# MLP weight factors of a fast pair made in place in its two raw buffers, in another order

## The chip, the cores and the metric

The kernel runs on one core of a Trainium2 chip. The time is that of one execution on the device in microseconds (us). It was measured three times for the kernel before: 2042.0, 2046.69 and 2047.65 us, with a median of 2046.69. Next to these stands one execution that was profiled.

Engine names in the profile: PE is TensorE (matmuls), PEld its weight loads, DVE is VectorE, ACT is ScalarE, POOL is GpSimd and SP is SyncE, which issues the loads. L145 is line 145 of the kernel.

## What is computed

A trunk of two layers over 256 tokens of width 2048. The first has a gated short convolution as its mixer, the second a latent attention; each is followed by a squared-ReLU MLP, and every part ends in a layer norm of the weighted residual sum. The change lies in the MLPs alone:

```python
def sq_relu_mlp(x, w1, w2):
    return jnp.square(jax.nn.relu(x @ w1)) @ w2

for layer in range(DEPTH):            # 2
    ...
    h = layer_norm(ALPHA * h + mix, ln_g[layer, 0], ln_b[layer, 0])
    h = layer_norm(ALPHA * h + sq_relu_mlp(h, mlp_w1[layer], mlp_w2[layer]),
                   ln_g[layer, 1], ln_b[layer, 1])
```

`w1` is 2048 x 8192 and `w2` 8192 x 2048, both float32.

## The kernel before

**Number form.** TensorE works on rounded floats (`F32R`). A float32 weight tile is therefore split in two: `hi` is the rounded value (a cast on ScalarE, L144), `lo` is the rest (source minus `hi`, on VectorE, L145). The function `split` does both. A product of two split operands is three matmuls (`dot`, L296 to L298): hi by hi, lo by hi, hi by lo.

**The stream of weights.** All weights of the kernel come in one list, `stream`, in the order of their use. An entry of kind "unit" is one tile of 128 x 1024 (512 KB). `prepare(i)` makes entry i ready: it loads it into a raw buffer (`load_raw`, a DMA on SyncE's queue, L165) and splits it into a pair of hi and lo buffers (`parts`). There are RAW = 5 raw buffers of 4 KB per partition and WA = 8 pairs of hi and lo. `take` hands out the next entry and first runs `prepare` so far that eight slots are ahead; a unit fills one slot, a plain pair two, a fast pair three.

**The second product of the MLP.** For 28 of the 32 pairs of K tiles (K is the 8192-wide inner dimension), `h @ w2` is made by a seven-product scheme for 2 x 2 blocks, in two column halves b = 0 and 1. A *fast pair* is one K tile pair in one half. Its weights come as two tiles: the first holds the blocks 11 and 22, the second 21 and 12. From them four factors are made:

- T1 = b12 - b11 and T3 = b12 - b22, in one VectorE instruction of 1024 columns into a third raw buffer `t` (L195)
- T2 = b22 - T1, in place of b12 (L197)
- T4 = b21 - T2, in place of b11, once b11 has been split (L199)

The tiles (11, 22), (T1, T3) and (21, T2) are then split into one hi/lo slot each, and T4 by itself into a tile `t4_i` of the tag "t4", which has two buffers of 4 KB. The three `yield` of `prepare` are the borders of the three slots. 92 pairs are fast, 46 in each layer; the others (`PLAIN`) are used as they are, with eight products and two slots.

**Seven sums in PSUM banks.** `FAST` lists the products as (sum, left factor, right factor), and a group of 21 matmuls runs them in that order; `PLAINS` does the same for a plain pair, with sums 3, 1, 2, 4 first. The sums 1 to 7 stay in seven PSUM banks while pairs of one half follow one another. After every four pairs the other half is taken up: `turn` spills each bank to SBUF (`spill`, ScalarE copy, L585) and puts the other half's sum back (`seed`, ScalarE copy, L589), bank by bank in the order of `FAST`, 1 3 7 5 2 6 4. With a plain pair next, bank 1 gets the sum "C" instead. The eighth bank is the only one left for the next item.

**Between the pairs**, one block of `x @ w1` (two units, 32 matmuls L231 and L235 into `ps_m`) is made after each group. ScalarE and VectorE empty it (`whole`, L337 and L338); after every second one they apply ReLU and square (L723, L659), form sums of blocks (L666 to L669) and split the result (`hc`, `ha`).

**What sets the order.** The source is one program order. A planner in the compiler draws up the queue of each engine from it: an instruction is placed when, by the planner's costs, its inputs are there, its buffer has been given back and its engine is free, earlier ones of the program first. [...] A buffer of a tag is given back when the last instruction that reads it has run.

Of the kernel before, what the change touches and what calls it, by code (L numbers as in the profile page):

```python
# [9 lines left out]
F32 = mybir.dt.float32  # L10
F32R = mybir.dt.float32r
AF = mybir.ActivationFunctionType
ALU = mybir.AluOpType
AX = mybir.AxisListType

P = 128
# [12 lines left out]
RMS_EPS = 1e-6  # L29
SCALE = (128 + 64) ** -0.5  # L30
NEG = -1e30
RAW, WA = 5, 8
NB = 4
BW = D // NB
PAIRS = FF // (2 * P)
# [13 lines left out]
def trunk(ctx: ExitStack, tc: tile.TileContext, xT, vecs, w_in, w_out, w_kv, w_q, w_uk, w_uv,  # L49
          w_qn, w_qp, w_o, w1, w2, w2f, cosT, sinT, mask, ident, gb, out):  # L50
    nc = tc.nc
# [3 lines left out]
    raws = ctx.enter_context(tc.tile_pool(name="raws", bufs=RAW))  # L55
# [83 lines left out]
    state = {"made": 0, "next": 0}  # L139
    ready = {}  # L140

    def split(hi, lo, src):

        nc.scalar.copy(hi, src)  # L144
        nc.vector.tensor_tensor(lo, src, hi.bitcast(F32), ALU.subtract)  # L145

    def tiled(w):
        return w.rearrange("p (b c) -> p b c", c=P)

    def parts(i):  # L150
        return tuple(whl.tile([P, 8, P], F32R, tag=t, name=f"{t}{i}") for t in ("hi", "lo"))
# [11 lines left out]
    def load_raw(i, src):  # L163
        raw = raws.tile([P, 1024], F32, tag="raw", name=f"raw{i}")
        nc.sync.dma_start(raw, src)  # L165
        return raw

    def prepare(i):

        kind, *src = stream[i]  # L170
        if kind == "unit":
            raw = load_raw(i, src[0])
            hi, lo = ready[i] = parts(i)
            split(hi, lo, tiled(raw))
            yield
            return
        r1, r2 = (load_raw(f"{i}_{j}", v) for j, v in enumerate(src))

        def finished(r, name):
            w = parts(f"{i}_{name}")  # L180
            split(*w, tiled(r))
            return [[v.rearrange("p b c -> p (b c)")[:, o:o + BW] for v in w] for o in (0, BW)]

        b11, b22, b21, b12 = r1[:, :BW], r1[:, BW:], r2[:, :BW], r2[:, BW:]
        out = {}
        if kind == "plain":
            out["11"], out["22"] = finished(r1, 1)
            yield
            out["21"], out["12"] = finished(r2, 2)
            ready[i] = out  # L190
            yield
            return
        t = raws.tile([P, 1024], F32, tag="raw", name=f"raw{i}_t")
        two = "p (a c) -> p a c"
        nc.vector.tensor_tensor(t.rearrange(two, a=2), b12.unsqueeze(1).to_broadcast([P, 2, BW]),  # L195
                                r1.rearrange(two, a=2), ALU.subtract)
        nc.vector.tensor_tensor(b12, b22, t[:, :BW], ALU.subtract)  # L197
        out["11"], out["22"] = finished(r1, 1)
        nc.vector.tensor_tensor(b11, b21, b12, ALU.subtract)  # L199
        yield  # L200
        out["T1"], out["T3"] = finished(t, "t")
        yield
        out["21"], out["T2"] = finished(r2, 2)
        f = state["fast"].tile([P, 2, BW], F32R, tag="t4", name=f"t4_{i}", bufs=2)
        split(f[:, 0, :], f[:, 1, :], b11)
        out["T4"] = [f[:, 0, :], f[:, 1, :]]
        ready[i] = out
        yield

    def all_steps():  # L210
        for i in range(2 * GROUP, len(stream)):
            yield from prepare(i)
# [319 lines left out]
    for m in range(NC):  # L532
        part = []
        for what in "cub":
            ps = next(pss)
            f = cbuf[:, m % 2, "cub".index(what), :T]
            whole(ps, f)
            part.append(f)
            if what == "u":
# [4 lines left out]
                y = cbuf[:, m % 2, 4, :T]  # L544
# [5 lines left out]
        if m >= NC // 2:  # L550
# [3 lines left out]
    ln.widen("a1", "a2")  # L554
    summed(ln, products(NC, z), residual)

    FAST = (("1", "11", "11"), ("3", "S4", "22"), ("7", "S3", "T3"), ("5", "S1", "T1"),
            ("2", "12", "21"), ("6", "S2", "T2"), ("4", "22", "T4"))
    PLAINS = (("3", "12", "22"), ("1", "22", "22"), ("2", "11", "11"), ("4", "21", "11"),
              ("3", "11", "12"), ("1", "21", "12"), ("2", "12", "21"), ("4", "22", "21"))  # L560

    class Sums:
# [30 lines left out]
        def group(self, b, w, x, plain, last, turns):  # L593
            forms = PLAINS if plain else FAST
            done = [p for p, _, _ in forms]
            for i, (p, l, r) in enumerate(forms):
                new = p not in self.live
                if p not in self.bank:
                    pool = pmm if p < "5" else Banks.more
                    self.bank[p] = pool.tile([P, 512], F32, tag="mm", name=f"sum{p}")  # L600
                dot(self.bank[p], w[r], x[l], new,
                    p not in done[i + 1:] and (last or p == "1" and turns), True)
                self.live[p] = (b, "C" if p == "1" and plain else p)

        def turn(self, b, plain):

            for p, _, _ in FAST:
                if p in self.bank:
                    self.spill(p)
                    self.seed(p, (b, "C" if p == "1" and plain else p))  # L610
# [184 lines left out]
    with tc.tile_pool(name="att", bufs=1) as ap:  # L795
# [61 lines left out]
        f = tmp.tile([P, T], F32, tag="fh", name="fpe", bufs=3)  # L857
# [28 lines left out]
        with tc.tile_pool(name="att2", bufs=2) as a2, \  # L886
# [73 lines left out]
            def attention(g, box):  # L960
                gens = [attend(4 * g + j, box) for j in range(4)]
                for step in range(6):
                    for j in range(3, -1, -1):
                        if 0 <= step - j < 3:
                            next(gens[j])
                            yield
# [14 lines left out]
            for g in range(5):  # L981
                box = {}
                a = attention(g - 1, prev) if prev is not None else iter(())
# [147 lines left out]
```

## Time and profile before

| | |
|---|---|
| runs (us) | 2042.0, 2046.69, 2047.65; median 2046.69 |
| profiled execution (us) | 2041.95 |
| its span (us) | 2040.0 |
| TensorE busy | 2003.0 us, 98% of the span |
| weight loads busy | 1740.1 us, 85% |
| VectorE busy | 1717.1 us, 84% |
| ScalarE busy | 1386.8 us, 68% |
| DMA | 385.31 MB, mean 189 GB/s |

The span runs from the first to the last instruction of the program. Busy times are unions, so overlapping instructions of one engine count once. A matmul's end is modelled, and matmuls overlap: a busy TensorE is not one at its peak, and the distance from one start to the next says more than the duration. Rows of groups read: line, engine, operation, output <- inputs, shape, count | busy us, mean ns of one | idle us of that engine just before them, and what ended most of it. Rows of waits read: who waited <- whom: us in all, times, longest. Idle time of an engine that is not the bottleneck costs nothing by itself.

### The profile page before, as it was taken

To read this page: it belongs to the slowest core of one execution; us is meant where nothing else is said; L and a number is where in the kernel's file an instruction comes from. 1 tells how busy PE (TensorE), PEld (TensorE's weight loads), DVE (VectorE), ACT (ScalarE), POOL (GpSimd) and SP (SyncE) were. 2 spreads that over 40 slices of the span, in tenths; PEclk is the share of its full clock that TensorE was granted. 3 is DMA by queue.
4 is the path that set the end of the run, shared out by engine and by line. 5 is a ranking of instruction groups with operands and counts; after the bars stand their busy time and mean duration, and the time that the engine had idled before them with its cause. 6 is when DMAs were issued, how large, how long until landed. Compare 5 with 4: busy or idle time off the path is not lost.

```text
span 2040.0 us, 30047 instructions
## 1 busy us (share of the span) xinstructions
PE 2003.0 (98%) x11088; PEld 1740.1 (85%) x11088; DVE 1717.1 (84%) x2483; ACT 1386.8 (68%) x2071; POOL 2.3 (0%) x21
## 2 busy tenths in 40 slices
PE   9999999999999999999999999999999999999997
PEld 8888888988888888888889998898788888888886
DVE  7667677799889898898878888779898988989886
ACT  6444444687887788877756655568777788787761
POOL 0000000000000000000000000000000000000000
PEclk9999999999999999999999999999999999999999
DMA  8655556455565665665754544655656666666672
GB/s 300 206 191 189 189 187 187 158 175 194 188 204 190 203 202 181 200 202 187 238 174 150 167 128 125 202 164 160 203 190 206 197 197 191 197 203 191 201 236 102
DMA packets 108003, 385.31 MB, mean 189 GB/s; under 512 B 11984, under 2 KB 13392, under 8 KB 107856
## 3 DMA queue, kind: packets, MB, share of 16 engines
q1 hardware_dynamic: 107712, 383.13, 58.1%
q8 instruction: 87, 1.43, 0.3%
q14 instruction: 60, 0.49, 0.1%
q10 hardware_dynamic: 144, 0.26, 0.0%
HBM read 381.25 MB, written 2.10 MB: 188 GB/s over the span
## 4 chain that ended last, share of the span: by engine, by line
PE 61%; DVE 18%; DMA 10%; ACT 6%; issue 4%; DVEq 0%; SPq 0%; ACTq 0%
PE ps_u L231 13%; PE ps_m L231 9%; DMA raw<-in_w2f_dram 9%; PE ps_u L235 7%; DVE lo L145 6%; PE ps_m L235 4%; PE sum L296 3%; PE sum L298 3%; PE sum L297 3%; ACT hi L144 3%; DVE raw_t L195 2%; DVE lo_t L145 2%; DVE ha L145 2%; PE ps_d L296 1%; PE ps_d L298 1%
## 5 line engine op out<-in xcount | busy, mean ns | idle before, releaser
L145 DVE TENSOR_TENSOR lo<-raw,hi 128x1024 fp32r<-128x1024 f32 x712 | 857.0, 1220 | 173.4 <-ACT hi L144 92.2
L144 ACT CAST hi<-raw 128x1024 fp32r<-128x1024 f32 x712 | 743.6, 1053 | 374.3 <-PE ps_u L231 157.7
L231 PE MATMUL ps_m<-xhl,hi 128*128 128x512 f32 x1792 | 455.1, 393 | 2.9 <-DVE sf L338 2.8
L231 PEld LDWEIGHTS ps_m<-xhl,hi 128*128 128x128 f32 x1792 | 330.1, 189 | 70.6 <-DVE sf L338 6.2
L235 PEld LDWEIGHTS ps_m<-xhl,lo 128*128 128x128 f32 x1792 | 245.2, 190 | 18.1
L235 PE MATMUL ps_m<-xhl,lo 128*128 128x256 f32 x1792 | 250.9, 282 | 0.0
L296 PE MATMUL sum<-hi,hc 128*128 128x512 f32 x512 | 202.6, 396 | 7.3 <-ACT sum L589 7.3
L297 PE MATMUL sum<-lo,hc 128*128 128x512 f32 x512 | 200.7, 392 | 0.0
L298 PE MATMUL sum<-hi,ha 128*128 128x512 f32 x448 | 173.3, 390 | 0.0
L231 PE MATMUL ps_u<-xhl_a,hi 128*128 128x512 f32 x720 | 172.0, 391 | 0.0
L144 ACT CAST hi_t<-raw_t 128x1024 fp32r<-128x1024 f32 x92 | 97.0, 1055 | 93.4 <-DVE raw_t L195 85.0
L231 PEld LDWEIGHTS ps_u<-xhl_a,hi 128*128 128x128 f32 x720 | 132.4, 188 | 25.7
L195 DVE TENSOR_TENSOR raw_t<-raw,raw 128x1024 f32<-128x1024 f32 x92 | 112.5, 1223 | 46.9 <-DMA raw<-in_w2f_dram 46.2
L296 PEld LDWEIGHTS sum<-hi,hc 128*128 128x128 f32 x512 | 96.6, 189 | 29.7 <-ACT sum L589 13.0
L585 ACT COPY sums<-sum 128x512 f32<-128x512 f32 x204 | 118.5, 587 | 3.5 <-PE sum L298 2.6
L589 ACT COPY sum<-sums 128x512 f32<-128x512 f32 x186 | 111.5, 599 | 1.4
L145 DVE TENSOR_TENSOR lo_t<-raw_t,hi_t 128x1024 fp32r<-128x1024 f32 x92 | 112.1, 1219 | 0.0
L297 PEld LDWEIGHTS sum<-lo,hc 128*128 128x128 f32 x512 | 96.7, 189 | 15.3
L298 PEld LDWEIGHTS sum<-hi,ha 128*128 128x128 f32 x448 | 84.2, 188 | 18.5
L235 PEld LDWEIGHTS ps_u<-xhl_a,lo 128*128 128x128 f32 x720 | 92.3, 191 | 3.5
L235 PE MATMUL ps_u<-xhl_a,lo 128*128 128x256 f32 x720 | 93.4, 283 | 0.0
L296 PE MATMUL sum<-hi_t,hc 128*128 128x512 f32 x168 | 66.5, 396 | 10.5 <-ACT sum L589 10.4
(241 smaller groups left out, 3315.7 us busy)
## 6 DMA issues: line engine op xcount, KB each, us to landing
raw<-in_w_dram SPq DMA_DIRECT2D x288, 512.0 KB, 4.5
raw<-in_w2f_dram SPq DMA_DIRECT2D x224, 512.0 KB, 4.0
raw<-in_w_in_dram SPq DMA_DIRECT2D x90, 512.0 KB, 4.3
raw<-in_w_out_dram SPq DMA_DIRECT2D x32, 512.0 KB, 4.0
raw<-in_w_o_dram SPq DMA_DIRECT2D x32, 512.0 KB, 3.7
raw<-in_w_kv_dram SPq DMA_DIRECT2D x10, 512.0 KB, 3.9
raw<-in_w_q_dram SPq DMA_DIRECT2D x8, 512.0 KB, 4.3
raw<-in_w_uk_dram SPq DMA_DIRECT2D x8, 512.0 KB, 4.4
```

What stands on the lines that cost most here:

```text
L144: nc.scalar.copy(hi, src)
L145: nc.vector.tensor_tensor(lo, src, hi.bitcast(F32), ALU.subtract)
L195: nc.vector.tensor_tensor(t.rearrange(two, a=2), b12.unsqueeze(1).to_broadcast([P, 2, BW]), r1.rearrange(two, a=2), ALU.subtract)
L231: nc.tensor.matmul(ps, w[blk // 8][0][:, blk % 8, :], x, start=first, stop=False)
L235: nc.tensor.matmul(ps[:, :T], w[blk // 8][1][:, blk % 8, :], x[:, :T], start=False, stop=last)
L296: nc.tensor.matmul(ps, x[0], w[0], start=first, stop=False, skip_group_check=goes_on)
L297: nc.tensor.matmul(ps, x[0], w[1], start=False, stop=False, skip_group_check=goes_on)
L298: nc.tensor.matmul(ps, x[1], w[0], start=False, stop=last, skip_group_check=goes_on)
L585: nc.scalar.copy(self.slot(self.live.pop(p)), self.bank[p])
L589: nc.scalar.copy(self.bank[p], self.at(key))
```

## The change

The four factors are made without the third raw buffer, by four subtractions of 512 columns, all after the split of the first tile:

- T1 = b12 - b11 in place of b11, T3 = b12 - b22 in place of b12, T2 = b22 - T1 in place of b22; these stand in the first slot's share of the program
- (T1, T2) is split from the first tile's buffer; then T4 = b21 - T2 in place of b11 and its split; these are the second slot's share
- (21, T3) is split from the second tile's buffer in the third slot's share

The tag "t4" has one buffer instead of two, and there are six raw buffers instead of five; the SBUF in use stays the same. The products of a fast group run in the order 1 3 5 6 4 2 7, and a turn goes by the same order if a fast pair is next, and by 1 3 4 2 5 6 7 if a plain one is.

```diff
-RAW, WA = 5, 8
+RAW, WA = 6, 8
...
-        t = raws.tile([P, 1024], F32, tag="raw", name=f"raw{i}_t")
-        two = "p (a c) -> p a c"
-        nc.vector.tensor_tensor(t.rearrange(two, a=2), b12.unsqueeze(1).to_broadcast([P, 2, BW]),
-                                r1.rearrange(two, a=2), ALU.subtract)
-        nc.vector.tensor_tensor(b12, b22, t[:, :BW], ALU.subtract)
+        minus = lambda o, x, y: nc.vector.tensor_tensor(o, x, y, ALU.subtract)
         out["11"], out["22"] = finished(r1, 1)
-        nc.vector.tensor_tensor(b11, b21, b12, ALU.subtract)
+        minus(b11, b12, b11)
+        minus(b12, b12, b22)
+        minus(b22, b22, b11)
         yield
-        out["T1"], out["T3"] = finished(t, "t")
-        yield
-        out["21"], out["T2"] = finished(r2, 2)
-        f = state["fast"].tile([P, 2, BW], F32R, tag="t4", name=f"t4_{i}", bufs=2)
+        out["T1"], out["T2"] = finished(r1, "t")
+        minus(b11, b21, b22)
+        f = state["fast"].tile([P, 2, BW], F32R, tag="t4", name=f"t4_{i}", bufs=1)
         split(f[:, 0, :], f[:, 1, :], b11)
         out["T4"] = [f[:, 0, :], f[:, 1, :]]
+        yield
+        out["21"], out["T3"] = finished(r2, 2)
         ready[i] = out
         yield
...
-    FAST = (("1", "11", "11"), ("3", "S4", "22"), ("7", "S3", "T3"), ("5", "S1", "T1"),
-            ("2", "12", "21"), ("6", "S2", "T2"), ("4", "22", "T4"))
+    FAST = (("1", "11", "11"), ("3", "S4", "22"), ("5", "S1", "T1"), ("6", "S2", "T2"),
+            ("4", "22", "T4"), ("2", "12", "21"), ("7", "S3", "T3"))
...
-            for p, _, _ in FAST:
+            for p in "1342567" if plain else [p for p, _, _ in FAST]:
                 if p in self.bank:
                     self.spill(p)
                     self.seed(p, (b, "C" if p == "1" and plain else p))
```

## The prediction

> **What bounds the kernel now.** I read the busy time of each engine by stretches (engines in the order PE, PEld, DVE, ACT, POOL, then TensorE's clock, the DMA share and GB/s), then who waits for whom.
>
> ```profile
> 440.00:1010.00 570.00, 558.54 (x2826) 471.27 (x2825) 517.26 (x623) 445.02 (x628) 0.00 (x0) 1.00 0.60 197
> ...
> 1390.00:1975.00 585.00, 575.35 (x2913) 486.33 (x2912) 529.97 (x636) 460.65 (x653) 0.00 (x0) 1.00 0.62 198
> ...
> PE sum L296 <- ACT sum L589: 18.0, 18, 2.5
> PE ps_m L231 <- DVE sf L338: 2.8, 2, 2.3
> ```
>
> These two stretches are the fast products of the two MLPs, where the edited code runs. TensorE idles there 570.0 - 558.5 = 11.5 and 585.0 - 575.4 = 9.7 us, and nearly all of it has two names: the first matmul of a product waiting for ACT to put a sum back into its bank (18.0 us in 18 waits), and a w1 product waiting for VectorE to empty its one bank (2.8 in 2). Weights are not named there. TensorE is the bound, and can save little more than these waits.
>
> A wait costs more than its idle time, as the timeline shows (start, duration, engine, line, idle time before in brackets):
>
> ```profile
> 810.54 0.39 PE L298 MATMUL sum<-hi_t,ha 128*128 128x512 f32 x1
> 812.85 0.50 PE L296 MATMUL sum<-hi_t,hc 128*128 128x512 f32 x1 [1.92 <-ACT sum L589]
> 813.18 0.40 PE L297 MATMUL sum<-lo_t,hc 128*128 128x512 f32 x1
> 813.42 0.39 PE L298 MATMUL sum<-hi_t,ha 128*128 128x512 f32 x1
> ...
> 480.00:520.00 40.00, 37.70 (x188) 31.83 (x187) 34.51 (x44) 31.41 (x45) 0.00 (x0) 0.96 0.63 203
> 1440.00:1480.00 40.00, 36.99 (x178) 30.73 (x177) 34.23 (x42) 30.47 (x43) 0.00 (x0) 0.96 0.58 188
> ```
>
> Undisturbed, a 512-column matmul starts about 0.23 us after the one before (813.18 to 813.42 is 0.24). At this wait 2.31 pass instead of 0.23, and then 0.33: 0.26 more than the 1.92 idle. For 20 waits that is 5.2 us. In two stretches of 40 us the granted clock is 0.96: 0.04 x 40 = 1.6 us each, 3.2 together. **Ceiling** of what waits can give back: 18.0 + 2.8 + 5.2 + 3.2 = 29 us.
>
> Why is ACT late? Its timeline in that wait, and the busy times and waits of a steady stretch of the first MLP, 520 to 1000 us (total us, times, longest):
>
> ```profile
> 810.50 1.05 ACT L144 CAST hi<-raw 128x1024 fp32r<-128x1024 f32 x1 [0.96 <-PE sum L298]
> 811.45 0.58 ACT L585 COPY sums<-sum 128x512 f32<-128x512 f32 x1
> ...
> 812.19 0.60 ACT L589 COPY sum<-sums 128x512 f32<-128x512 f32 x1
> ...
> 520.00:1000.00 480.00, 471.00 (x2385) 397.29 (x2384) 434.37 (x515) 380.92 (x539) 0.00 (x0) 1.00 0.61 198
> ...
> ACT hi L144 <- DMA raw<-in_w2f_dram: 23.3, 25, 2.3
> DVE raw_t L195 <- DMA raw<-in_w2f_dram: 20.8, 24, 2.1
> DVE lo L145 <- ACT hi L144: 16.8, 27, 1.5
> ...
> ACT hi L144 <- PE ps_m L231: 7.0, 9, 1.2
> ...
> SPq L165 <- DVE lo L145: 168.1, 97, 5.6
> SPq L165 <- DVE lo_t L145: 142.1, 33, 6.4
> ```
>
> The seed that TensorE wants ends at 812.8, behind a cast that itself waited and a spill, in one queue. In 480 us ACT is busy 380.9 and VectorE 434.4, and both lose time to the same thing: w2 tiles that have not landed (23.3 and 20.8 us). The loads are late because SyncE waits for VectorE to give raw buffers back. So the loop behind ACT's lateness is the five raw buffers.
>
> **The change part by part.**
>
> *VectorE's arithmetic.*
>
> ```profile
> L195 DVE TENSOR_TENSOR raw_t<-raw,raw 128x1024 f32<-128x1024 f32 x92 | 112.5, 1223 | 46.9 <-DMA raw<-in_w2f_dram 46.2
> L145 DVE TENSOR_TENSOR lo_t<-raw_t,hi_t 128x1024 fp32r<-128x1024 f32 x92 | 112.1, 1219 | 0.0
> L199 DVE TENSOR_TENSOR raw<-raw 128x512 f32<-128x512 f32 x92 | 63.3, 688 | 1.4
> L197 DVE TENSOR_TENSOR raw<-raw,raw_t 128x512 f32<-128x512 f32 x92 | 63.2, 687 | 1.2
> L145 DVE TENSOR_TENSOR t<-raw,t 128x512 fp32r<-128x512 f32 x92 | 63.0, 685 | 1.6 <-ACT t L144 1.6
> L144 ACT CAST hi_t<-raw_t 128x1024 fp32r<-128x1024 f32 x92 | 97.0, 1055 | 93.4 <-DVE raw_t L195 85.0 <-PE ps_m L231 5.4 <-PE ps_m L235 2.5
> L144 ACT CAST t<-raw 128x512 fp32r<-128x512 f32 x92 | 57.3, 623 | 7.1 <-DVE raw L199 7.1
> ```
>
> Per fast pair it removes one 1024-wide subtraction and two 512-wide (1.223 + 0.687 + 0.688 = 2.598 us) and adds four 512-wide of the same form (4 x 0.688 = 2.752): +0.154 us, x92 = +14.2 us of VectorE's time. The cover is VectorE's idle time: 480.0 - 434.4 = 45.6 us in the steady stretch, against 38 pairs x 0.154 = 5.9 (38: the 92 pairs shared out over the 570 + 585 us by time). On the path: 0. If the cover were gone it would cost the whole 14.2. Splits stay as they are in number and size; so do DMAs and matmuls.
>
> *Raw buffers.* Before, a step (fast pair plus one w1 block) takes 3 + 2 = 5 of 5 raw buffers; after, 2 + 2 = 4 of 6.
>
> ```profile
> 494.68 0.40 PE L296 MATMUL sum<-hi,hc 128*128 128x512 f32 x1
> ...
> 499.46 1.98 PE L231 MATMUL ps_m<-xhl,hi 128*128 128x512 f32 x8
> ...
> 505.02 0.40 PE L296 MATMUL sum<-hi,hc 128*128 128x512 f32 x1
> ...
> 829.05 1.22 DVE L195 TENSOR_TENSOR raw_t<-raw,raw 128x1024 f32<-128x1024 f32 x1
> ...
> 835.46 0.69 DVE L145 TENSOR_TENSOR t<-raw,t 128x512 fp32r<-128x512 f32 x1
> ...
> raw<-in_w2f_dram SPq DMA_DIRECT2D x224, 512.0 KB, 4.0
> ```
>
> TensorE takes 505.02 - 494.68 = 10.34 us a step, 4.78 of it the pair's. So a buffer comes round every 10.34 us now and every 10.34 x 6 / 4 = 15.5 after. Less 4.0 for the transfer, that leaves 6.3 us of holding now; the first buffer of a pair is held 829.05 to 836.15, 7.1. In the new order that buffer's whole chain is cast, lo, three subtractions, cast, lo, subtraction, cast and lo of T4: 1.055 + 1.219 + 3 x 0.688 + 1.055 + 1.219 + 0.688 + 0.623 + 0.685 = 8.6 us, against 11.5 allowed. I expect the waits on w2 loads (20.8 on VectorE, 23.3 on ACT) to go nearly to nothing. That is no saving in itself; it lets both engines run ahead of TensorE as far as the eight hi/lo buffers let them, so that the copies of a turn find a shorter queue.
>
> *T4's single buffer.* The next pair's T4 may now be written only after this pair's product 4.
>
> ```profile
> 815.81 0.69 DVE L145 TENSOR_TENSOR t<-raw,t 128x512 fp32r<-128x512 f32 x1
> ...
> 820.03 0.40 PE L298 MATMUL sum<-t,ha 128*128 128x512 f32 x1
> ...
> 825.56 0.39 PE L296 MATMUL sum<-t,hc 128*128 128x512 f32 x1
> ```
>
> Here T4 is written 9.75 us before its use and 4.6 us before the other buffer's last read ends (820.43). With one buffer it waits these 4.6, less about 1.4, as product 4 moves two products up (2 of 7 x 4.78). Some 5 us of lead remain. On the path 0 then. From above: a wait for something that TensorE frees costs 7.0 / 9 = 0.78 us where ACT meets one now; 38 of them are 30 us, within the 480 - 381 = 99 that ACT has idle. I take 0, since the lead covers it; behind such a wait stand the next casts, and a turn's copies.
>
> *Order of products and of the turn.* Before, a turn into a plain pair moved banks 1 3 7 5 2 6 4, though that pair's third and fourth products use 2 and 4. Now 4 is third and 2 fourth. The waits by operand:
>
> ```profile
> L296 PE MATMUL sum<-hi,hc 128*128 128x512 f32 x512 | 202.6, 396 | 7.3 <-ACT sum L589 7.3
> L296 PE MATMUL sum<-hi_t,hc 128*128 128x512 f32 x168 | 66.5, 396 | 10.5 <-ACT sum L589 10.4
> ...
> L585 ACT COPY sums<-sum 128x512 f32<-128x512 f32 x204 | 118.5, 587 | 3.5 <-PE sum L298 2.6
> L589 ACT COPY sum<-sums 128x512 f32<-128x512 f32 x186 | 111.5, 599 | 1.4
> ```
>
> Spill and seed of a bank take 0.587 + 0.599 = 1.19 us, so bank 4 comes four pairs of copies (4.7 us) earlier and bank 2 one (1.2). Plain pairs have only hi operands, so their waits lie in the 7.3; I count 5 of it as gone. The 10.4 on hi_t belong to fast pairs, whose banks are still moved in the order of use; there only ACT's lead helps, and I count half, 5. From the 2.8 on the evacuation and the 3.2 of clock I count half, 3. With them go about 11 waits at 0.26, 3. **Sum:** -(5 + 5 + 3 + 3) = -16 us, between 0 (a new order of queues that waits as much) and -29 (the ceiling).
>
> [...]
>
> The profiled execution took 2041.95 us, its span 2040.0. The median of the runs, 2046.69, is 4.7 above it, and the profiled one is as low as the lowest (2042.0). So 2041.95 - 16 = 2026 for a run like the profiled one, and 2046.69 - 16 = 2030.7 for the median. I forecast 2030.
>
> **The rivals.** *B, slower: VectorE waits for ACT inside the pair.* Before, the subtraction of T1 and T3 needed only landed tiles, and lo of the pair's first tile stood between it and lo_t, which never waited (0.0 in its row). After, VectorE must do lo, subtract, wait for ACT's cast of T1 and T2 (1.055), do lo, subtract, wait for the cast of T4 (0.623). If nothing else stands between, that is up to 1.68 us per pair. For it: both queues are in order, as the seed behind the cast shows, and VectorE is busy 434.4 of 480. Against it: a step has other VectorE work to put there, and now that 4 of 6 buffers are used it has mostly landed; today's 27 waits of a lo for its cast come to only 16.8 us in the stretch. Price with the first cast uncovered: 434.4 + 5.9 + 38 x 1.055 + half of the 24.8 of today's idle time that isn't DMA (45.6 - 20.8) = 492.8, 12.8 over 480; per pair 0.34, x92 = +31, so 2078. It decides once 0.4 to 1.0 us per pair is uncovered ((45.6 - 5.9 - 24.8) / 38 and (45.6 - 5.9) / 38).
>
> [...]
>
> *C, no change.* The loads come early, but the turn's copies queue as before: 14 copies are 7 x 1.19 = 8.3 us in a step of 10.34, whatever has landed. At 810.50 ACT waited for TensorE and not for a load, which speaks for it. The queues are drawn up anew, and new waits take back what the plain pairs gain: 2045.
>
> *D, the ceiling.* ACT runs far enough ahead that all 29 us go: 2046.7 - 29.2 = 2017.5.
>
> **How the numbers follow.** Forecast 0.48, D 0.10, B 0.29, C 0.13. The forecast's own range is 2013 to 2040: from D less the 4.7 by which runs lie under the median, to a gain of 6. The whole range reaches to B's price: 2013 to 2078. Faster by over 0.3% (6 us, about what a measurement of this kernel tells from no change): 0.48 + 0.10 = 0.58; within it C, 0.13; slower B, 0.29.
>
> **What would show it.** Right: no DMA named ahead of VectorE's subtractions or ACT's casts in the fast stretches; SyncE's waits there named after hi/lo work shorter; TensorE's waits for the seeds under 10 us, those on hi operands near 2; VectorE 14 us busier. Wrong by B: lo of T1 and T2 waiting for ACT with over 0.5 us each, and VectorE's idle time in the steady stretches no less than 45. Wrong by C: the seeds' 18 us unchanged although the loads are no longer named. T4 is wrong if casts or lo of t wait for TensorE's L298. A w1 product waiting for VectorE's L338 more than 3 us in all would mean that the evacuation is the next to be late.

## The result, and the profile after

The changed kernel takes 2032.16 us (median of four runs, 2031.37 to 2033.02); beside it the kernel before took 2045.14 (four runs). The ratio is 0.9937, 95% interval 0.992 to 0.9955: faster by 13 us, 0.63%. The profiled execution took 2031.37, its span 2029.6, 10.4 less than before.

Busy times of the two fast stretches, the two stretches of 40 us in which the clock had dropped (columns as in the prediction), and all that TensorE waited for in the edited code:

```profile
440.00:1010.00 570.00, 565.81 (x2868) 474.99 (x2867) 525.33 (x669) 446.88 (x632) 0.00 (x0) 1.00 0.58 198
1390.00:1975.00 585.00, 579.61 (x2955) 487.55 (x2953) 535.89 (x674) 458.96 (x649) 0.00 (x0) 1.00 0.58 198
...
480.00:520.00 40.00, 39.38 (x202) 33.10 (x201) 36.40 (x45) 33.66 (x48) 0.00 (x0) 1.00 0.58 203
1440.00:1480.00 40.00, 39.66 (x200) 33.29 (x200) 36.38 (x47) 33.17 (x49) 0.00 (x0) 1.00 0.59 208
...
PE sum L295 <- ACT sum L588: 5.1, 10, 0.5
PE ps_m L230 <- DVE sf L337: 2.2, 1, 2.2
PE sum L296 <- DVE lo L145: 1.0, 2, 0.6
PE ps_m L230 <- ACT hi L144: 0.8, 1, 0.8
```

TensorE's idle time in the two stretches fell from 21.1 to 4.2 + 5.4 = 9.6 us, and the clock no longer drops (granted 1.00 in both stretches of 40 us, 0.96 before). Seeds are waited for 5.1 us instead of 18.0, never over 0.5. That is 11.5 of idle time and 3.2 of clock (an estimate, 0.04 x 40 in each of the two stretches), 14.7 in all, and the span shrank by 10.4. From the start of the first product matmul (`sum`) to that of the last, the two MLPs take 574.9 and 574.0 us instead of 583.1 and 579.6, 13.8 less. The rest of the program takes 3.4 more; 2.9 of it are TensorE's two waits just behind the last products, the 2.2 and the 0.8 above (at 1949.55 and 990.07). The remaining waits for seeds all stand before products with hi operands, and weight loads (PEld) now come late for want of a lo:

```profile
L295 PE MATMUL sum<-hi,hc 128*128 128x512 f32 x512 | 196.8, 396 | 5.2 <-ACT sum L588 5.1
L295 PE MATMUL sum<-hi_t,hc 128*128 128x512 f32 x168 | 65.4, 389 | 0.0
L296 PEld LDWEIGHTS sum<-lo,hc 128*128 128x128 f32 x512 | 96.5, 189 | 23.5 <-DVE lo L145 8.4
L145 DVE TENSOR_TENSOR lo_t<-raw,hi_t 128x1024 fp32r<-128x1024 f32 x92 | 112.7, 1225 | 68.5 <-ACT hi_t L144 68.5
L193 DVE TENSOR_TENSOR raw<-raw,raw 128x512 f32<-128x512 f32 x276 | 189.3, 686 | 3.0
```

The fourth row is the new wait: before lo of (T1, T2), VectorE stands idle 68.5 us, 0.74 per pair, until ScalarE has cast them. The fifth (with a fourth subtraction of 690 ns) is the arithmetic as priced. Now the busy times and the waits of the steady stretch, and SyncE's own:

```profile
520.00:1000.00 480.00, 476.48 (x2405) 399.20 (x2405) 440.96 (x555) 381.99 (x540) 0.00 (x0) 1.00 0.58 198
...
DVE lo_t L145 <- ACT hi_t L144: 29.7, 38, 1.1
...
DVE lo L145 <- ACT hi L144: 2.2, 9, 0.3
...
SPq L165 <- DVE lo L145: 217.7, 108, 8.5
...
raw<-in_w2f_dram SPq DMA_DIRECT2D x224, 512.0 KB, 5.7
```

No wait for a w2 load is left among VectorE's and ScalarE's, though such a load now lands 5.7 us after its issue instead of 4.0 and SyncE still waits for VectorE before it issues: the loads land before their use. VectorE's idle time is 39.0 us of 480; 29.7 of them are the new wait. In VectorE's timeline, and then in ScalarE's:

```profile
809.70 0.69 DVE L193 TENSOR_TENSOR raw<-raw 128x512 f32<-128x512 f32 x1
811.50 1.23 DVE L145 TENSOR_TENSOR lo_t<-raw,hi_t 128x1024 fp32r<-128x1024 f32 x1 [1.11 <-ACT hi_t L144]
...
816.65 0.68 DVE L145 TENSOR_TENSOR t<-raw,t 128x512 fp32r<-128x512 f32 x1
...
805.62 1.05 ACT L144 CAST hi<-raw 128x1024 fp32r<-128x1024 f32 x1
...
810.42 1.05 ACT L144 CAST hi_t<-raw 128x1024 fp32r<-128x1024 f32 x1 [1.27 <-DVE raw L193]
811.38 1.05 ACT L144 CAST hi<-raw 128x1024 fp32r<-128x1024 f32 x1
```

Each waits for the other: ScalarE 1.27 us for the last subtraction, then VectorE 1.11 for the cast. The last line of VectorE is lo of T4, with which the first raw buffer of the pair is given back; its cast to hi, by the order of the program, is the one at 805.62.

### The profile page after: what moved, and what is told of

Its sections match the earlier page's. It is cut to its first block, busy times and chain, and to the rows that moved or that the text cites. A ratio compares the mean times of both kernels' runs of the same rounds, so it can differ in the third digit from the quotient of the medians.

```text
span 2029.6 us, 29846 instructions
## 1 busy us (share of the span) xinstructions
PE 2004.9 (99%) x11088; PEld 1735.4 (86%) x11088; DVE 1729.8 (85%) x2575; ACT 1384.2 (68%) x2071; POOL 2.3 (0%) x21
## 3 DMA queue, kind: packets, MB, share of 16 engines
q8 instruction: 87, 1.43, 0.3%
## 4 chain that ended last, share of the span: by engine, by line
PE 61%; DVE 17%; ACT 14%; issue 5%; DMA 2%; DVEq 0%; ACTq 0%; SPq 0%
PE ps_u L230 13%; PE ps_m L230 9%; PE ps_u L234 7%; DVE lo L145 7%; PE ps_m L234 5%; DVE raw L193 4%; ACT hi L144 4%; PE sum L296 3%; PE sum L297 3%; PE sum L295 3%; ACT sums L584 2%; ACT hi_t L144 2%; DVE lo_t L145 2%; ACT sum L588 2%; DMA raw<-in_w_dram 1%
## 5 line engine op out<-in xcount | busy, mean ns | idle before, releaser
L144 ACT CAST hi<-raw 128x1024 fp32r<-128x1024 f32 x712 | 726.2, 1050 | 261.2 <-PE ps_u L230 158.1
L230 PE MATMUL ps_m<-xhl,hi 128*128 128x512 f32 x1792 | 449.3, 391 | 3.0 <-DVE sf L337 2.2
L295 PE MATMUL sum<-hi,hc 128*128 128x512 f32 x512 | 196.8, 396 | 5.2 <-ACT sum L588 5.1
L193 DVE TENSOR_TENSOR raw<-raw,raw 128x512 f32<-128x512 f32 x276 | 189.3, 686 | 3.0
L144 ACT CAST hi_t<-raw 128x1024 fp32r<-128x1024 f32 x92 | 96.6, 1050 | 113.5 <-DVE raw L193 113.4
L145 DVE TENSOR_TENSOR lo_t<-raw,hi_t 128x1024 fp32r<-128x1024 f32 x92 | 112.7, 1225 | 68.5 <-ACT hi_t L144 68.5
L722 ACT ACTIVATE sf<-sf 128x512 f32<-128x512 f32 x56 | 35.4, 631 | 57.2 <-DVE sf L337 57.2
```

Of the source, the lines that this page charges most:

```text
L193: minus = lambda o, x, y: nc.vector.tensor_tensor(o, x, y, ALU.subtract)
L230: nc.tensor.matmul(ps, w[blk // 8][0][:, blk % 8, :], x, start=first, stop=False)
L295: nc.tensor.matmul(ps, x[0], w[0], start=first, stop=False, skip_group_check=goes_on)
L722: nc.scalar.activation(f[:, :4 * P], f[:, :4 * P], AF.Relu)
```

## The experiments

Theory A: the gain comes from the raw buffers (loads in time). Theory B: it comes from the orders of turns and products. P: factors in place cost something, since VectorE waits for ScalarE's cast. O: the new order of products costs it. Each kernel was timed beside the kernel before; differences below are differences of ratios times 2043 us.

| run | edit | median us | ratio to before, interval |
|---|---|---|---|
| after | the change | 2032.16 | 0.9937, 0.992 to 0.9955 |
| e1 | before, 6 raw, 1 T4 | 2026.79 | 0.9911, 0.9894 to 0.9928 |
| e2 | before, new turns | 2031.56 | 0.9942, 0.992 to 0.9964 |
| e3 | after, 5 raw | 2052.63 | 1.0037, 1.0024 to 1.0049 |
| e4 | after, turns by the fast order | 2032.05 | 0.9936, 0.9919 to 0.9953 |
| e5 | e1 and e2 together | 2046.5 | 1.0018, 1.0002 to 1.0034 |
| e6 | after, old products | 2031.51 | 0.9943, 0.9923 to 0.9963 |
| e7 | after, lo of T4 twice | 2083.14 | 1.0200, 1.0174 to 1.0225 |
| e8 | after, slots 2 and 3 exchanged | 2008.72 | 0.9835, 0.9811 to 0.9859 |
| e9 | before, lo of T4 twice | 2035.89 | 0.9958, 0.994 to 0.9977 |
| e10 | after, 5 raw, 2 T4 | 2052.02 | 1.0039, 1.0024 to 1.0053 |
| e11 | e8, 5 raw | 2018.14 | 0.9866, 0.9841 to 0.989 |
| e12 | e8, lo of T4 twice | 2034.56 | 0.9951, 0.9932 to 0.997 |

### Buffers alone, and orders alone

```diff
# e1, from before
-RAW, WA = 5, 8
+RAW, WA = 6, 8
-        f = state["fast"].tile([P, 2, BW], F32R, tag="t4", name=f"t4_{i}", bufs=2)
+        f = state["fast"].tile([P, 2, BW], F32R, tag="t4", name=f"t4_{i}", bufs=1)
# e2, from before
-            for p, _, _ in FAST:
+            for p in "1342567" if plain else [p for p, _, _ in FAST]:
```

> The kernel before with six raw buffers and one T4 buffer, nothing else changed: factors still made with a third buffer, old orders. Theory A (loads: the gain comes from w2 tiles that land in time, so that ScalarE's queue is ahead at a turn): a step takes 5 of 6 buffers, a round of 10.34 x 6 / 5 = 12.4 us instead of 10.34; about half of the 13 us gain, 2038, and VectorE's wait of the first subtraction for w2 loads falls from 46 us to under 15. Theory B (orders: the gain comes from the order in which banks are moved and products run): no change, 2045, and TensorE's wait for seeds stays near 18.

> The kernel before with the new order of a turn into a plain pair alone (1 3 4 2 5 6 7); buffers, factors and products as before. A: the waits before plain pairs go, 2 to 3 us in all, 2042, and the loads stay late (46 us). B: most of the gain, 2034, with TensorE's wait for seeds near 7.

Each by itself gains about as much as the whole change: 18 us with the buffers, 12 with the turns. Of e1:

```profile
PE sum L296 <- ACT sum L589: 13.1, 12, 2.3
...
DVE raw_t L195 <- DMA raw<-in_w2f_dram: 25.0, 27, 2.9
...
ACT hi L144 <- DMA raw<-in_w2f_dram: 3.6, 3, 1.8
```

The waits for loads about halve on VectorE (25.0 from 46.2, where A had under 15) and nearly go on ScalarE (3.6 from 59.9). That is A's direction; the gain is more than twice the half of 13 us that A gave it. Of e2, whole run:

```profile
PE sum L296 <- ACT sum L589: 16.0, 15, 2.1
...
ACT hi L144 <- DMA raw<-in_w2f_dram: 40.7, 37, 2.3
DVE raw_t L195 <- DMA raw<-in_w2f_dram: 39.5, 39, 2.8
```

Three quarters of the waits for loads are left (80.2 us of 106.1), and the seeds are waited for nearly as long, so neither theory explains its 12 us as told. What changed in both kernels, and in the changed one, is the head of each fast stretch. In the kernel before, TensorE waited there for an evacuation and for a seed, each wait followed by the dropped clock (granted 0.83 from 510 to 520 and from 1475 to 1485):

```profile
510.46 3.45 PE L231 MATMUL ps_m<-xhl,hi 128*128 128x512 f32 x8 [2.31 <-DVE sf L338]
...
1475.56 0.50 PE L296 MATMUL sum<-hi,hc 128*128 128x512 f32 x1 [2.53 <-ACT sum L589]
```

e1 has no wait at the first of these places and 1.69 us at the second, e2 has 0.81 and 0.80 at the first and 1.72 at the second, and the clock does not drop there in either (mean granted clock of the span 0.998 in e1 and 0.999 in e2, 0.997 in the kernel before). The 50 product matmuls around the stall took 32.3 and 33.3 us in the kernel before, 28.3 and 30.1 in e1, 30.3 and 30.4 in e2. So the heads give about 7 us of e1's 18 and 5 of e2's 12; the rest is not traced to a place.

### Parts taken back

```diff
# e3, from after
-RAW, WA = 6, 8
+RAW, WA = 5, 8
# e4, from after
-            for p in "1342567" if plain else [p for p, _, _ in FAST]:
+            for p, _, _ in FAST:
```

> The changed kernel with five raw buffers. A: a step takes 4 of 5, a round of 12.9 us, 8.9 of them for holding against 8.6 for the longest chain: loads begin to be late again, 2036. B: as the changed kernel, 2032.

> The changed kernel with every turn in the order of the fast products (1 3 5 6 4 2 7), also into a plain pair. A: bank 2 comes two pairs of copies (2.4 us) later for the plain pair; 2034, loads in time. B: the gain is gone, 2043, with TensorE's wait for seeds near 15.

Without its sixth buffer the change is a loss: 20 us slower than with it, 8 slower than the kernel before. The order of turns is worth nothing in the changed kernel. Of e3, whole run, the last row its steady stretch:

```profile
PE sum L295 <- ACT sum L588: 10.9, 26, 0.5
PE ps_m L230 <- ACT hi L144: 3.9, 1, 3.9
...
ACT hi L144 <- DMA raw<-in_w2f_dram: 11.7, 12, 1.1
...
DVE lo L145 <- ACT hi L144: 8.6, 15, 1.2
```

The waits for seeds are 26 instead of 10, with 10.9 us in all instead of 5.1, and there is one of 3.9 us at the end of the first fast stretch. ScalarE waits for loads again, and VectorE's other lo wait for their casts 8.6 us in the steady stretch instead of 2.2. If VectorE sets the pace there (next but one section), these 6.4 us in 480 are about 15 over the 1155 us of both stretches, an estimate that comes near the 20. So A holds for the changed kernel, with a larger size than it gave: factors in place need the sixth buffer. B falls there.

### Both together, and which part of the change costs

```diff
# e5, from before: the edits of e1 and of e2
# e6, from after: products as before
-    FAST = (("1", "11", "11"), ("3", "S4", "22"), ("5", "S1", "T1"), ("6", "S2", "T2"),
-            ("4", "22", "T4"), ("2", "12", "21"), ("7", "S3", "T3"))
+    FAST = (("1", "11", "11"), ("3", "S4", "22"), ("7", "S3", "T3"), ("5", "S1", "T1"),
+            ("2", "12", "21"), ("6", "S2", "T2"), ("4", "22", "T4"))
```

> Six raw buffers, one T4 buffer and the new order of turns with the old factors and products: the two edits that each gained 13 to 18 us by themselves, together. If they remove different waits: 2044.7 - 17.9 - 13.1 = 2014. If both remove the same long stalls at the start of each fast stretch (TensorE's 2.3 and 2.5 us waits and the drop of the clock after them): 2024 to 2028, no better than six buffers alone.

> The changed kernel with the products in the old order (1 3 7 5 2 6 4), turns into fast pairs likewise. Theory P (making the factors in place costs, since VectorE waits for ScalarE's cast of T1 and T2): as the changed kernel, 2032, with that wait still near 0.78 us per pair. Theory O (the order of the products costs the 5 us by which the changed kernel lies over the old factors with six buffers): 2027.

Neither expectation of e5 held: the two edits that gained 18 and 12 us gain nothing together, and it is 4 us slower than the kernel before, just clear of its interval. Waits of e5, and one stretch with its clock:

```profile
PE sum L296 <- ACT sum L589: 15.6, 15, 1.9
PE ps_m L231 <- DVE sf L338: 6.9, 10, 0.8
...
880.00:920.00 40.00, 37.35 (x182) 30.59 (x182) 35.96 (x46) 31.04 (x44) 0.00 (x0) 0.96 0.63 197
```

Nine turns into a fast pair now meet a wait for a seed of 0.4 to 1.9 us and one for the evacuation right behind (0.3 to 0.8), and the clock drops at six of them (the row shows one, 0.96 over its 40 us; the mean of the span is 0.993 against 0.997 before). The head stalls are gone here too, so they alone do not decide the time. Every edit makes the planner draw up all queues anew, and with the old factors the outcome of these edits lies anywhere from -18 to +4 us. In that family none of these numbers can be taken for the price of its edit. e6 is the changed kernel again, so O falls.

### Is VectorE's idle time cover?

```diff
# e7, from after (e9 likewise from before, e12 from e8)
         split(f[:, 0, :], f[:, 1, :], b11)
+        minus(f[:, 1, :], b11, f[:, 0, :].bitcast(F32))
```

> The changed kernel with the lo of T4 written twice, the same values: 0.685 us more of VectorE per pair, 63 us in all. If VectorE's idle time in the steady stretches (39 us of 480, 1.0 us per pair) is cover: 2032 to 2036, and VectorE's idle time falls to about 13 us of 480. If it is no cover, since the waits for ScalarE stand in a chain with it: 2032 + 63 = 2095, with the idle time unchanged.

> The kernel before with the lo of T4 written twice, the same values: 63 us more of VectorE. If VectorE's idle time was cover in the kernel before (45.6 us of 480, 20.8 of them waits for loads): 2043 to 2055. If VectorE with the loads that wait for it set the pace there already: 2043 + 50 = 2093, as in the changed kernel.

63 us of added VectorE time cost the changed kernel 54 us (1.0200 - 0.9937), and cost the kernel before nothing (it is 9 us faster, which was not expected: one more draw of the queues, as far as is known). Steady stretches of e7 and of e9, and TensorE's main wait in e7:

```profile
520.00:1000.00 480.00, 464.70 (x2304) 381.31 (x2303) 442.20 (x566) 367.49 (x518) 0.00 (x0) 1.00 0.55 188
...
PE sum L297 <- DVE lo L145: 20.6, 27, 1.3
```

```profile
520.00:1000.00 480.00, 472.63 (x2377) 397.42 (x2376) 451.14 (x552) 379.62 (x534) 0.00 (x0) 1.00 0.62 196
```

In e9 VectorE's busy time rises from 434.4 to 451.1 of 480: the idle time was cover. In e7 it stays at 442 while fewer matmuls fit in the stretch: the 38 us of idle time are not used. In the trace 27.5 of them are the wait before lo_t, in a chain of VectorE for ScalarE and ScalarE for VectorE. In the changed kernel VectorE with that wait sets the pace: its work (440.96) and its waits of lo for casts (29.7 and 2.2) make 472.9 of 480 us.

### The wait taken away

```diff
# e8, from after
+        out["21"], out["T3"] = finished(r2, 2)
+        yield
         out["T1"], out["T2"] = finished(r1, "t")
...
         out["T4"] = [f[:, 0, :], f[:, 1, :]]
-        yield
-        out["21"], out["T3"] = finished(r2, 2)
...
-    FAST = (..., ("5", "S1", "T1"), ("6", "S2", "T2"), ("4", "22", "T4"), ("2", "12", "21"), ("7", "S3", "T3"))
+    FAST = (..., ("2", "12", "21"), ("7", "S3", "T3"), ("5", "S1", "T1"), ("6", "S2", "T2"), ("4", "22", "T4"))
```

> The changed kernel with slots two and three exchanged: (21, T3) is split before (T1, T2) and T4, and the products run 1 3 2 7 5 6 4. ScalarE's cast of (21, T3) and VectorE's lo of it stand where VectorE waited for the cast of T1 and T2. P: that wait falls from 30 us to under 10 in a steady stretch, and the time by 5 to 8, to 2025. O: nothing is gained by it, 2032.

2008.72 us, 21 us faster than the changed kernel and 34 faster than the one before (ratio 0.9835, 0.9811 to 0.9859): the best of all. Of e8, VectorE and then ScalarE around one pair, the steady stretches, and the waits for casts:

```profile
821.63 0.69 DVE L193 TENSOR_TENSOR raw<-raw 128x512 f32<-128x512 f32 x1
822.71 1.23 DVE L145 TENSOR_TENSOR lo<-raw,hi 128x1024 fp32r<-128x1024 f32 x1 [0.39 <-ACT hi L144]
823.85 1.22 DVE L145 TENSOR_TENSOR lo_t<-raw,hi_t 128x1024 fp32r<-128x1024 f32 x1
...
821.63 1.05 ACT L144 CAST hi<-raw 128x1024 fp32r<-128x1024 f32 x1 [4.21 <-DVE raw L193]
822.59 1.05 ACT L144 CAST hi_t<-raw 128x1024 fp32r<-128x1024 f32 x1
...
520.00:1000.00 480.00, 480.00 (x2463) 409.78 (x2462) 453.05 (x565) 386.82 (x545) 0.00 (x0) 1.00 0.60 204
1480.00:1960.00 480.00, 480.00 (x2473) 410.13 (x2472) 450.87 (x564) 383.51 (x543) 0.00 (x0) 1.00 0.61 208
...
DVE lo L145 <- ACT hi L144: 15.5, 38, 0.9
DVE lo_t L145 <- ACT hi_t L144: 3.0, 13, 0.2
```

(21, T3) needs two subtractions, not three, so ScalarE casts it during the third, and VectorE's lo of it stands where VectorE had waited. The wait before lo_t falls from 29.7 to 3.0 us. A shorter one comes instead, before lo of (21, T3) (0.39 us in the timeline), so that the waits of lo for casts rise from 2.2 to 15.5; together they fall from 31.9 to 18.5 us. That is enough: TensorE has no idle time left in either steady stretch, 480.00 of 480.00, with 2463 matmuls instead of 2405. This is P, with about three times the size that was expected (21 us against 5 to 8). The waits saved, 13.4 us in 480, would make some 32 over both stretches (x 1155 / 480, an estimate) if VectorE still set the pace; the gain stops at 21, where TensorE has no idle time left.

### Which buffer, and what is left

```diff
# e10, from after: RAW = 5, bufs=2 for "t4"
# e11, from e8: RAW = 5
# e12, from e8: lo of T4 twice
```

> The changed kernel with five raw buffers and two T4 buffers: the factors in place and the new orders, but the buffers of the kernel before. If the single T4 buffer holds the first raw tile until product 4 of the pair before has run, and the sixth buffer only makes up for that: 2032 to 2040, against 2052.6 with five and one. If raw buffers are short by themselves: 2050.

> Slots two and three exchanged, with five raw buffers and one T4 buffer. If the sixth buffer is what brings the loads in time: 2025 to 2035, and TensorE waits at turns again. If taking VectorE's wait for the cast of T1 and T2 away is enough: 2009 to 2013.

> Slots two and three exchanged, with the lo of T4 written twice (63 us more of VectorE, which then has about 480 of 480 us to do in a steady stretch: 453 + 38 x 0.685 = 479). If VectorE's remaining idle time is cover now: at most 2025, a quarter of the 63. If a chain of waits still goes through VectorE: 2060.

e10 equals e3: with five raw buffers a second T4 buffer gives nothing, raw buffers are short by themselves. e11 lies between its two expectations: the sixth buffer is worth about 6 us with the exchange (0.9866 - 0.9835; the two intervals overlap) and 20 without it. In e12 24 of the 63 us are seen, 38%: more than the quarter that cover was to cost (2025 expected, 2034.56 measured), and far less than the 54 of e7. VectorE is busy 460.39 of 480 us there, and TensorE waits for lo again (6.8 us in 22 waits):

```profile
PE sum L297 <- DVE lo L145: 6.8, 22, 0.4
...
520.00:1000.00 480.00, 475.99 (x2401) 398.55 (x2400) 460.39 (x592) 385.13 (x538) 0.00 (x0) 1.00 0.58 197
```

## Why the prediction held, point by point

**Direction and size.** Forecast -16 us and 2030, measured -13 and 2032.16: within the likeliest case's own range. But that the sum came out is in part luck: its terms were off in both directions, and a cost that it put at nothing, VectorE's wait for the cast, was there.

**Raw buffers: right in the main, and too small.** The waits for w2 loads went from 20.8 and 23.3 us to nothing, as forecast. The holding time was not 8.6 us: in the timeline above the first buffer is held some 11.7 from the start of its cast (805.62 to 817.33), more than the 11.5 allowed, as waits and other work stand between; loads were in time all the same. SyncE waited as long as before, some 418 us of 480 against 424, a good part of it now for the subtractions; the sign of shorter waits after hi/lo work holds only if these are left out. The prediction gave this only a part of its 16 us; by e3 the sixth buffer is worth 20 in this kernel. And it is the sixth buffer that pays: with the old factors (e1) the products of both MLPs take 1149.9 us from first to last, in the changed kernel 1148.9, against 1162.7 before. Making the factors in place, with the new orders, gained nothing beside it; by the medians e1 is even 5 us faster.

**VectorE's arithmetic: duration right, cover wrong.** Four subtractions of 686 to 690 ns stand in for 2.598 us, as priced; VectorE is 12.7 us busier in all (1729.8 against 1717.1), where 14.2 were priced. The step "on the path: 0", because 45.6 us of VectorE were idle, most likely failed: e9 shows that this was cover in the kernel before, e7 that in the changed kernel 54 of 63 added us show. By that share the 14.2 us cost about 12; this was not measured by itself.

**Rival B's mechanism was there, and its account was incomplete.** The wait for the cast of T1 and T2 came as told (29.7 us of 480, 0.78 per pair, inside the 0.4 to 1.0 at which it was to decide); the forecast priced it at nothing. Of B's two signs the wait of over 0.5 us was there, the idle time of at least 45 was not (39.0). The kernel is faster all the same, since waits for loads (20.8) and most waits of other lo for their casts (16.8 to 2.2) went at the same time. e8 gives a price, 21 us for taking 13.4 of these waits' 31.9 us out of the steady stretch. As to the order of VectorE's queue, the seed behind the cast showed ScalarE's alone; the same stretch of the kernel before has a case on VectorE: it stood idle 1.43 us for a load until L195 at 806.32, and the lo at 807.46, whose cast was over by 805.20, came only after that. In the changed kernel VectorE stood idle 1.11 us before lo_t at 811.50, and a new program order (e8) filled such gaps (3.0 us in the steady stretch instead of 29.7).

**T4's single buffer: right.** No cast or lo of T4 waited for TensorE by more than 0.3 us in all, and e10 against e3 puts the second buffer at nothing, with five raw buffers.

**Turns: wrong in the split.** Of the 7.3 us on hi operands 5 were to go by the plain pairs' order: 2.2 went (5.1 are left, where the prediction wanted near 2), and the order is worth nothing (e4). Of the 10.4 on hi_t half was to go, by ScalarE's lead: all went. The two errors partly cancel. The new order of products, for which the sum had no term, is worth nothing (e6). The 3 us for what a wait costs beyond its idle time are not seen: the products became 13.8 us shorter, idle time and clock alone would make 14.7.

**Heads of the stretches and the clock: more than half.** Both drops went (granted clock 1.00 instead of 0.96 in both stretches of 40 us), 3.2 us by the estimate above, where half was counted. Before the two drops TensorE had stood idle 2.31 and 2.53 us; the last section has drops behind shorter waits (1.93 and 1.84 us). The evacuation hardly gained: 2.8 us before, 2.2 after, now behind the last product of the second MLP.

**Rival C** had the copies' order on ScalarE untouched by the loads. It fell: the longest wait for a seed went from 2.5 to 0.5 us. Its second half, that the queues are drawn up anew and can take the gain back, is what e5 shows for the old factors.

**Open.** Why the old factors give -18 and -12 us for the two edits and +4 for both was traced only in part, to places (heads of the stretches, turns into fast pairs), and not to the planner's choices.

## What to carry to other kernels

Idle time of an engine is no cover when it is a wait in a chain that sets the pace (e7: 54 of 63 added us showed), and can be where it isn't (e9: none of the 63 showed): ask for each gap whether the engine could have run something else from its queue, and test it with a harmless extra instruction. Where two engines hand a tile to and fro and wait for each other (here 1.27 and 1.11 us), put an independent tile between the two handovers; here exchanging two slots gained as much (21 us) as the sixth buffer (20). Where a compiler draws up the queues, a small edit's gain in one version says little about the same edit in another: measure it in the version that will be kept.

## What was not expected of the hardware

The clock dropped behind short waits of TensorE, and not behind all of them. In e5 it dropped (granted 0.96 from 880 to 920) behind waits that were no longer than 1.93 us singly, when further waits stood close by; in e1 it dropped (0.91 from 840 to 860) behind one wait of 1.84 us that stood alone (no other within 40 us). Lines of e5, then of e1:

```profile
894.95 0.50 PE L296 MATMUL sum<-hi_t,hc 128*128 128x512 f32 x1 [0.45 <-ACT sum L589]
...
897.85 0.62 PE L296 MATMUL sum<-hi_t,hc 128*128 128x512 f32 x1 [1.93 <-ACT sum L589]
898.26 0.63 PE L297 MATMUL sum<-lo_t,hc 128*128 128x512 f32 x1
...
847.40 0.50 PE L296 MATMUL sum<-hi,hc 128*128 128x512 f32 x1 [1.84 <-ACT sum L589]
...
840.00:860.00 20.00, 18.16 (x86) 14.95 (x85) 15.78 (x17) 17.29 (x26) 0.00 (x0) 0.91 0.49 140
```

In e5, 0.45 and 1.93 us stand 2.9 us apart; from 898.26 a matmul starts 0.43 us after the one before instead of 0.23. The length of a wait does not decide by itself: the wait of 1.92 us at 812.85 in the kernel before stood alone and was not followed by a drop (granted 1.00 from 800 to 840), nor was that of 2.15 us at 1949.55 in the changed kernel, with one of 0.28 us 15 us ahead of it (1.00 from 1940 to 1960). Those of 2.11 and 2.29 us in e1 (761.58 and 1720.88) stood alone and were not followed by one either: e1's mean clock, 0.998 with the drop at 847.40, lies between the 0.997 of the kernel before, with two drops, and the 0.999 of the changed kernel, without one in its fast stretches. Company is not needed, as the 1.84 us of e1 show. What does decide is open.
